# Sums of the normed x from its two parts, and another order of products in the first layer

## The chip, the cores and the metric

The kernel runs on one core of a Trainium2 chip. The time is device microseconds of one execution, the median of three runs. The profile is of one further execution, whose own time is given below. The engines are called as in the profile: PE is TensorE, PEld its weight load, DVE VectorE, ACT ScalarE, POOL GpSimd, SP SyncE.

## The reference

Two layers on 256 positions of width 1024 in fp32. Each layer has two feed-forward steps (ffa, ffb) with a mixer (attention) between them, and a last norm follows. The change is in the feed-forward steps:

```python
def rms_norm(x, g):
    y = xf * lax.rsqrt(jnp.mean(xf * xf, axis=-1, keepdims=True) + EPS)
    return (y * g.astype(jnp.float32)).astype(x.dtype)

def swiglu(x, w_gate, w_up, w_down):
    return (jax.nn.silu(x @ w_gate) * (x @ w_up)) @ w_down

for l in range(DEPTH):
    x = x + 0.5 * swiglu(rms_norm(x, ffa_norm[l]), ffa_w_gate[l], ffa_w_up[l], ffa_w_down[l])
    x = x + hybrid_mixer(rms_norm(x, mix_norm[l]), ...)
    x = x + 0.5 * swiglu(rms_norm(x, ffb_norm[l]), ffb_w_gate[l], ffb_w_up[l], ffb_w_down[l])
return rms_norm(x, final_norm)
```

The gate and up matrices are 1024 x 2816, the down matrix is 2816 x 1024.

## The kernel before

Every fp32 operand is split in a high and a low part. The high part is a rounded copy that ScalarE makes (whi at L300, xhi at L413, hhi at L557), the low part is the rest, which VectorE subtracts (wlo at L279, xlo at L416, hlo at L559). A product is then three matmuls of 128x512 (L319 to L321): high with high, low with high, high with low.

The feed-forward steps run in the order ffa0, ffb0, ffa1, ffb1, with mix0 and mix1 behind ffa0 and ffa1. "Layer 0" in this document is ffa0, the first of them. At the start of each, x is transposed on TensorE (L407) 128x128 at a time into a bank of PSUM (tb). ScalarE makes xhi from it and VectorE xlo. The kernel also needs the normed x (its gain included, its row factor not) as four plain fp32 blocks of 128x512, called a11, a12, a21, a22. ScalarE copies them out of the same bank by 128x128 (L428), into tiles called p, 16 copies for each of the four steps. Two such blocks are added or subtracted on VectorE (L527), and the results are split again (L531, L533) into "forms" for products 5, 6, 3 and 7.

The gate and up columns are worked in an order that a plan per step gives. A name g0, u0, g2 and so on is a plain block of 512 columns of gate or up, in two halves of the depth (16 products in all); h5 is the last block, 256 columns of each. A name of two digits is one of seven Strassen-like products, the first digit, of a pair of column blocks, the second digit; it has four products. The weights of these are sums, too: products 1, 5, 6, 4 of a column follow each other in one raw tile (3 and 7 in another), and each step adds the next matrix to it by an accumulating DMA from POOL (adder, L255 to L262). Such a DMA may start only when the split of the one before is over. Product 43 is thus 63's tile with one more gate block added. After the plan come the 11 units of the down matrix (d0 to d10).

A planner, class Flow, builds the program: threads ask for events, buffers and times, and it steps whichever is due first by a rough model of the engines' times. What it emits is the program's order, and every engine runs its own list in that order. The splitter (L264 to L298) takes the weights unit by unit, in halves, up to three units ahead of TensorE, since there are six pairs of whi and wlo halves. There are five raw tiles, five p tiles, two tb banks.

The norm's squares (L442) are taken by ScalarE from x, and their factor is computed by VectorE (L346 to L357) and applied later, at the gate.

Of the kernel before, what the change touches and what calls it, by code (L numbers as in the profile page):

```python
# [8 lines left out]
F32 = mybir.dt.float32  # L9
# [3 lines left out]
AF = mybir.ActivationFunctionType  # L13
OP = mybir.AluOpType
AX = mybir.AxisListType

T = 2
D = 1024
KT = D // 128
# [20 lines left out]
ARRIVE = [4.4, 5.2, 6.7, 7.4], [8.9, 9.6, 11.1, 11.8]  # L40
ARRIVE_X = [3.5, 5.9, 8.1, 10.3]
HOP = 0.3
PLANS = ("g0 u0 11 g2 51 21 31 u2 61 71 13 g4 41 53 23 33 u4 63 73 h5 43".split(),) * 4
AC = 0.1
DV = 0.06

# [84 lines left out]
def hybrid_kernel(ctx, tc, x_in, ffa_norm, ffa_w_gate, ffa_w_up, ffa_w_down, mix_norm, w_in,  # L131
# [3 lines left out]
    nc = tc.nc  # L135
# [10 lines left out]
    fl = Flow()  # L146
    NRAW, NW, NP = 5, 6, 5
# [7 lines left out]
    def tbank():  # L155
        return bank("tb", 2)
# [4 lines left out]
    def md(shape, name, bufs):  # L161
        return mid.tile(shape, F32, name=name, tag=name, bufs=bufs)
# [10 lines left out]
    class Raw:  # L173


        def __init__(self, src, a, b, loads=1):
            self.src, self.a, self.b, self.loads = src, a, b, loads
            self.landed = [Event() for _ in range(4)]
            raws.append(self)
# [198 lines left out]
    class Norm:  # L378

        def __init__(self, gi, wide=False, plain=False):
            self.gi, self.wide = gi, wide
            self.xs = (big.tile([128, KT, 256], F32R, name="xhi", tag="xhi"),
                       big.tile([128, KT, 256], F32R, name="xlo", tag="xlo"))
            self.rs = small.tile([128, T], F32, name="rs", tag="rs", bufs=4)
            self.ss = small.tile([128, 2, T], F32, name="ss2", tag="ss2")
            if wide:
                self.rsb = mid.tile([128, 256], F32, name="rsb", tag="rsb", bufs=1)
            self.plain = {} if plain else None  # L390
            self.turned = {(k, t): Event() for k in range(KT) for t in range(T)}
            self.scaled, self.spread = Event(), Event()
            self.plained, self.left = Event(), KT * T
            self.count = 0

        def gain(self, k):
# [2 lines left out]
        def turn(self, ks, ts, e=0.0):  # L399

            yield e
            yield fl.get("tb")
            ps = tbank()
            n = 128 * len(ts)
            for i, k in enumerate(ks):
                for t in ts:
                    nc.tensor.transpose(ps[:, i * n + (t - ts[0]) * 128:i * n + (t - ts[0] + 1) * 128],  # L407
                                        x[:, t, k * 128:(k + 1) * 128], ident)
            yield fl.pe(0.44)
            sl = slice(ts[0] * 128, ts[0] * 128 + n)  # L410
            es = []
            for i, k in enumerate(ks):
                nc.scalar.activation(self.xs[0][:, k, sl], ps[:, i * n:(i + 1) * n], AF.Copy, scale=self.gain(k))  # L413
                es.append(fl.act(n))
            for i, k in enumerate(ks):
                nc.vector.scalar_tensor_tensor(self.xs[1][:, k, sl], ps[:, i * n:(i + 1) * n], self.gain(k),  # L416
                                               self.xs[0][:, k, sl].bitcast(F32), op0=OP.mult, op1=OP.subtract)
                e = fl.dve(n, es[i])
                for t in ts:
                    self.turned[k, t].set(e)  # L420
            if self.plain is not None:
                for i, k in enumerate(ks):
                    for t in ts:
                        if (t, k // 4) not in self.plain:
                            yield fl.get("p")
                            self.plain[t, k // 4] = md([128, 512], "p", NP)
                        b = i * n + (t - ts[0]) * 128
                        nc.scalar.activation(self.plain[t, k // 4][:, k % 4 * 128:(k % 4 + 1) * 128],  # L428
                                             ps[:, b:b + 128], AF.Copy, scale=self.gain(k))
                        e = max(e, fl.act(128))  # L430
                        self.left -= 1
                if not self.left:
                    self.plained.set(e)
            fl.put("tb", 0, e)

        def squares(self, t, c, e=0.0):
# [61 lines left out]
    def ffn(us, nm, nxt, plan, last=False):  # L498
# [8 lines left out]
        def event(*k):  # L507
            return evs.setdefault(k, Event())
# [6 lines left out]
        def sums():  # L515

            for k in range(KT):
                for t in range(T):
                    yield nm.turned[k, t]
            yield nm.plained  # L520
            a11, a12, a21, a22 = (nm.plain[t, c] for t in range(T) for c in range(2))
            ho, lo = ([big.tile([128, 4, 256], F32R, name="f" + z, tag=z).rearrange(
                "p a b -> p (a b)").rearrange("p (f n) -> p f n", f=2) for z in tags]
                for tags in (("nhi", "ohi"), ("nlo", "olo")))
            for o, p, q, op in ((a22, a22, a21, OP.subtract), (a21, a11, a21, OP.subtract),
                                (a11, a22, a11, OP.add), (a12, a11, a12, OP.subtract)):
                nc.vector.tensor_tensor(o, p, q, op)  # L527
                yield fl.dve(512)
            for i, (f, z) in enumerate((("5", a22), ("6", a11), ("3", a12), ("7", a21))):
                h, l = ho[i // 2][:, i % 2], lo[i // 2][:, i % 2]  # L530
                nc.scalar.activation(h, z, AF.Copy)  # L531
                yield fl.act(512)
                nc.vector.tensor_tensor(l, z, h.bitcast(F32), OP.subtract)  # L533
                e = fl.dve(512)
                fl.put("p", 0, e)
                forms[f] = [y.rearrange("p (k c) -> p k c", k=4) for y in (h, l)]
                event("form", f).set(e)
# [915 lines left out]
    def finish(t, c, box, g):  # L1453
        if c == 0:
            box["ss"] = small.tile([128, 2], F32, name="ss", tag="ss")
        ss = box["ss"]
        yield fl.get("p")
        junk = md([128, 512], "p", NP)
        nc.scalar.activation(junk, x[:, t, c * 512:(c + 1) * 512], AF.Square, accum_out=ss[:, c:c + 1])
        e = fl.act(512, 0.2)  # L1460
        fl.put("p", 0, e)
        yield e
        if c == 0:
            return
        r = small.tile([128, 1], F32, name="rs1", tag="rs1", bufs=2)
        yield newton([ss[:, :1], ss[:, 1:]], D, r)
        for c in range(2):
            sl = slice(c * 512, (c + 1) * 512)
            yield fl.get("work")
            y = wk([128, 512], "y")  # L1470
            nc.vector.scalar_tensor_tensor(y, x[:, t, sl], r, g[c], op0=OP.mult, op1=OP.mult)
            yield fl.dve(512)
            (nc.sync, nc.scalar)[c].dma_start(out[0, t * 128:(t + 1) * 128, sl], y)
            fl.put("work")
# [6 lines left out]
    units = []  # L1481
    plans = iter(PLANS)
    for i, (kind, _, w) in enumerate(layers):
# [44 lines left out]
    def main():  # L1528
        for i, (kind, _, w) in enumerate(layers):
            last = i + 1 == len(layers)  # L1530
            box = {}

            def nxt(a, c, box=box, i=i, last=last):
                if last:
                    fl.spawn(finish(a, c, box.setdefault(a, {}), box["g"]))
                else:
                    if len(norms) < i + 2:
                        kind2, gi, _ = layers[i + 1]
                        norms.append(Norm(gi, kind2 == "mix", kind2 == "ff" and any(
                            z[0] in "1234567" for z in units[i + 1][1])))  # L1540
                    fl.spawn(norms[i + 1].pair(a, c))

            def gains_out(box=box):
                box["g"] = []
                for c in range(2):
                    yield fl.get("p")
                    g = md([128, 512], "p", NP)
                    nc.gpsimd.dma_start(g, bass.AP(tensor=final_norm.tensor, offset=final_norm.offset + 512 * c,
                                                   ap=[[0, 128], [1, 512]]))
                    box["g"].append(g)  # L1550

            if kind == "ff":
                us, plan = units[i]
                yield from ffn(us, norms[i], nxt, plan, gains_out if last else None)
            else:
                yield from mixer(w, units[i], norms[i], nxt)
            while not last and len(norms) < i + 2:
                yield fl.clock + 0.5
# [5 lines left out]
    def warm():  # L1564
# [5 lines left out]
            fl.pe(0.215)  # L1570
            yield fl.clock
        fl.put("acc")
    norms = [Norm(0, False, any(z[0] in "1234567" for z in units[0][1]))]
    fl.spawn(warm(), 9)
    fl.spawn(turn_gains(*gr))
    for q in range(4):
# [43 lines left out]
```

## Time and profile before

| | |
|---|---|
| median of three runs | 1027.48 us (1026.64 to 1027.61) |
| profiled execution | 1027.06 us, span 1025.3 us |
| granted TensorE clock, mean | 0.996 of full |
| PE, DVE, ACT busy | 97%, 71%, 61% of the span |

The page gives shares over the whole span. What the waits are worth is seen in the timeline of one engine, where each row has its start, its duration, and in brackets how long the engine was idle ahead of it and what ended that. Matmuls overlap, so the distance of two starts, not the duration, tells how fast they run.

### The profile page before, as it was taken

What the parts mean: (1) busy time and instruction counts of PE and PEld (TensorE: products, weight loads), DVE (VectorE), ACT (ScalarE), POOL (GpSimd) and SP (SyncE); (2) the same over time, 40 slices, a digit from 0 to 9 for tenths busy, and PEclk for the clock granted to TensorE, in tenths of its full rate; (3) what the DMA queues carried; (4) which work ended last, traced back from release to release, by engine and by line L of the source; (5) the groups of instructions that cost most, each with busy time, mean ns of one, the idle gap of its engine ahead of it and who ended that gap; (6) DMA issues with size and microseconds to landing.
All of it is one profiled execution on the core that took longest, in us unless ns stands there. A gap on an engine that the chain in (4) does not pass through costs nothing.

```text
span 1025.3 us, 14273 instructions
## 1 busy us (share of the span) xinstructions
PE 999.1 (97%) x5276; PEld 827.0 (81%) x5276; DVE 730.7 (71%) x1367; ACT 621.2 (61%) x1105; POOL 53.5 (5%) x61
## 2 busy tenths in 40 slices
PE   8999999999999999999989999999999989999996
PEld 6788888898876788888878888888978768788885
DVE  5978854688786868784477778447888768688544
ACT  7766543569575866653376566336795767665431
POOL 1110000100000010100001110001000001110000
PEclk9999999999999999999999999999999999999998
DMA  9799965363732599975539998653655237999611
GB/s 327 216 280 258 278 240 180 114 195 109 280 124 82 151 264 291 265 262 198 171 121 229 285 274 266 199 168 111 206 195 175 84 106 224 267 268 303 222 67 41
DMA packets 100983, 207.63 MB, mean 203 GB/s; under 512 B 3785, under 2 KB 23377, under 8 KB 100913
## 3 DMA queue, kind: packets, MB, share of 16 engines
q1 hardware_dynamic: 83072, 171.65, 48.3%
q0 software_dynamic: 17536, 34.54, 19.0%
q8 instruction: 41, 0.67, 0.3%
q10 hardware_dynamic: 304, 0.53, 0.1%
q14 instruction: 30, 0.24, 0.1%
HBM read 205.66 MB, written 1.05 MB: 202 GB/s over the span
## 4 chain that ended last, share of the span: by engine, by line
PE 80%; DVE 8%; ACT 5%; DMA 5%; issue 2%; DVEq 0%; POOL 0%; ACTq 0%; POOLq 0%
PE acc L319 16%; PE acc L320 15%; PE acc L321 15%; PE sb L319 6%; PE sb L321 6%; PE sb L320 6%; DVE wlo L279 3%; DMA raw<-in_ffb_w_up_dram 3%; PE acc L336 2%; PE acc L337 2%; PE acc L338 2%; DMA raw<-in_ffa_w_up_dram 2%; PE acc L1081 2%; PE tb L552 2%; PE tb L1063 2%
## 5 line engine op out<-in xcount | busy, mean ns | idle before, releaser
L279 DVE TENSOR_TENSOR wlo<-raw,whi 128x1024 fp32r<-128x1024 f32 (+2 forms) x404 | 449.8, 1138 | 191.0 <-ACT whi L300 190.4
L300 ACT ACTIVATE whi<-raw 128x1024 fp32r<-128x1024 f32 (+2 forms) x404 | 388.4, 989 | 240.3 <-PE acc L321 89.8
L319 PE MATMUL acc<-whi,hhi 128*128 128x512 f32 x352 | 138.5, 394 | 0.0
L321 PE MATMUL acc<-whi,hlo 128*128 128x512 f32 x352 | 137.4, 390 | 0.0
L320 PE MATMUL acc<-wlo,hhi 128*128 128x512 f32 x352 | 137.1, 390 | 0.0
L320 PE MATMUL acc<-wlo,xhi 128*128 128x512 f32 (+1 forms) x320 | 123.5, 386 | 7.5 <-DVE wlo L279 7.4
L319 PE MATMUL acc<-whi,xhi 128*128 128x512 f32 (+1 forms) x320 | 126.8, 396 | 1.4 <-ACT whi L300 1.4
L319 PE MATMUL sb<-whi,xhi 128*128 128x512 f32 x320 | 125.5, 392 | 0.0
L321 PE MATMUL sb<-whi,xlo 128*128 128x512 f32 x320 | 124.8, 390 | 0.0
L320 PE MATMUL sb<-wlo,xhi 128*128 128x512 f32 x320 | 124.7, 390 | 0.0
L321 PE MATMUL acc<-whi,xlo 128*128 128x512 f32 (+1 forms) x320 | 122.7, 383 | 0.1
L320 PEld LDWEIGHTS acc<-wlo,xhi 128*128 128x128 f32 x320 | 60.7, 190 | 20.7 <-DVE wlo L279 11.1
L321 PEld LDWEIGHTS acc<-whi,hlo 128*128 128x128 f32 x352 | 66.1, 188 | 13.9
L320 PEld LDWEIGHTS acc<-wlo,hhi 128*128 128x128 f32 x352 | 66.2, 188 | 13.4
L319 PEld LDWEIGHTS acc<-whi,hhi 128*128 128x128 f32 x352 | 66.1, 188 | 13.2
L319 PEld LDWEIGHTS acc<-whi,xhi 128*128 128x128 f32 x320 | 60.6, 189 | 12.4 <-ACT whi L300 1.9
L321 PEld LDWEIGHTS acc<-whi,xlo 128*128 128x128 f32 x320 | 60.5, 189 | 12.2 <-DVE xlo L416 0.9
L321 PEld LDWEIGHTS sb<-whi,xlo 128*128 128x128 f32 x320 | 60.1, 188 | 12.6
L320 PEld LDWEIGHTS sb<-wlo,xhi 128*128 128x128 f32 x320 | 60.1, 188 | 12.3
L319 PEld LDWEIGHTS sb<-whi,xhi 128*128 128x128 f32 x320 | 60.1, 188 | 12.2
L336 PE MATMUL acc<-xhi,whi 128*128 128x256 f32 x192 | 56.5, 294 | 0.0
L337 PE MATMUL acc<-xlo,whi 128*128 128x256 f32 x192 | 54.3, 283 | 0.0
(221 smaller groups left out, 1434.5 us busy)
## 6 DMA issues: line engine op xcount, KB each, us to landing
raw<-in_ffa_w_down_dram SPq DMA_DIRECT2D x22, 1024.0 KB, 5.1
raw<-in_ffb_w_down_dram SPq DMA_DIRECT2D x22, 1024.0 KB, 5.1
raw<-in_w_in_dram SPq DMA_DIRECT2D x20, 1024.0 KB, 5.1
raw<-in_ffb_w_gate_dram SPq DMA_DIRECT2D x20, 1024.0 KB, 5.2
raw<-in_ffa_w_gate_dram SPq DMA_DIRECT2D x18, 1024.0 KB, 7.7
raw<-in_ffa_w_up_dram SPq DMA_DIRECT2D x16, 1024.0 KB, 6.1
raw<-in_ffb_w_up_dram SPq DMA_DIRECT2D x16, 1024.0 KB, 7.0
raw<-in_ffa_w_up_dram POOLq DMA_DIRECT2D x12, 1024.0 KB, 9.2
```

The source lines that it names most:

```text
L279: nc.vector.tensor_tensor(view(u, lo, i, True), source(u, i), view(u, hi.bitcast(F32), i, True), OP.subtract)
L300: nc.scalar.activation(view(u, u.halves[-1][0], i, True), source(u, i), AF.Copy)
L319: nc.tensor.matmul(ps, xh, wh, start=first, stop=False, skip_group_check=True)
L320: nc.tensor.matmul(ps, xh, wl, start=False, stop=False, skip_group_check=True)
L321: nc.tensor.matmul(ps, xl, wh, start=False, stop=last, skip_group_check=True)
L336: nc.tensor.matmul(ps, wh, xs[0][:, k], start=first and j == 0, stop=False, skip_group_check=True)
L337: nc.tensor.matmul(ps, wh, xs[1][:, k], start=False, stop=False, skip_group_check=True)
L338: nc.tensor.matmul(ps, wl, xs[0][:, k], start=False, stop=last, skip_group_check=True)
L552: nc.tensor.transpose(ps[:, j * 128:(j + 1) * 128], h[:, j * 128:(j + 1) * 128], ident)
L1063: nc.tensor.transpose(ps[:, j * 128:(j + 1) * 128], pp[:, i * n + s_ * 128:i * n + (s_ + 1) * 128], ident)
L1081: nc.tensor.matmul(grp.o[u * 64:(u + 1) * 64, h // 2 * 128:(h // 2 + 1) * 128], val(s_), pT[:, j * 128:(j + 1) * 128], start=u not in grp. ...
```

## The change

ScalarE's 16 plain copies per step (L428 before) are gone, and with them the events that told when they were done. Instead, when all of x is split and the norm's factor is computed, VectorE adds xhi and xlo, 128x512 at a time, into the four p tiles (L514 after). The tb bank is released straight after xlo. The plan of layer 0 differs from that of the other three, where all four had been alike: g2 comes ahead of product 11, and the blocks u2, g4, u4 and h5 each take the place of the next, so that h5 stands ahead of 63.

```diff
-PLANS = ("g0 u0 11 g2 51 21 31 u2 61 71 13 g4 41 53 23 33 u4 63 73 h5 43".split(),) * 4
+PLANS = ("g0 u0 g2 11 u2 51 21 31 g4 61 71 13 u4 41 53 23 33 h5 63 73 43".split(),) + (
+    "g0 u0 11 g2 51 21 31 u2 61 71 13 g4 41 53 23 33 u4 63 73 h5 43".split(),) * 3
...
-            if self.plain is not None:
-                for i, k in enumerate(ks):
-                    for t in ts:
-                        if (t, k // 4) not in self.plain:
-                            yield fl.get("p")
-                            self.plain[t, k // 4] = md([128, 512], "p", NP)
-                        b = i * n + (t - ts[0]) * 128
-                        nc.scalar.activation(self.plain[t, k // 4][:, k % 4 * 128:(k % 4 + 1) * 128],
-                                             ps[:, b:b + 128], AF.Copy, scale=self.gain(k))
-                        e = max(e, fl.act(128))
-                        self.left -= 1
-                if not self.left:
-                    self.plained.set(e)
             fl.put("tb", 0, e)
...
-            yield nm.plained
-            a11, a12, a21, a22 = (nm.plain[t, c] for t in range(T) for c in range(2))
+            yield nm.scaled
+            yield fl.clock + 1.0
+            blocks = []
+            for t in range(T):
+                for c in range(2):
+                    yield fl.get("p")
+                    a = md([128, 512], "p", NP)
+                    h, l = (z[:, 4 * c:4 * c + 4, t * 128:(t + 1) * 128].bitcast(F32) for z in nm.xs)
+                    nc.vector.tensor_tensor(a.rearrange("p (k c) -> p k c", k=4), h, l, OP.add)
+                    yield fl.dve(512)
+                    blocks.append(a)
+            a11, a12, a21, a22 = blocks
```

The first place is ScalarE's list at the program's start, where g0's weights are split in pieces of 128x512 between the pieces of x. Before:

```order
L300 ACTIVATE whi<-raw 128x512
L413 ACTIVATE xhi<-tb,gall 128x256 x2
L428 ACTIVATE p<-tb,gall 128x128 x4
L300 ACTIVATE whi<-raw 128x512
L413 ACTIVATE xhi<-tb,gall 128x256 x2
L428 ACTIVATE p<-tb,gall 128x128 x4
L300 ACTIVATE whi<-raw 128x512 x2
L413 ACTIVATE xhi<-tb,gall 128x256 x2
L428 ACTIVATE p<-tb,gall 128x128 x4
L300 ACTIVATE whi<-raw 128x512 x2
L413 ACTIVATE xhi<-tb,gall 128x256 x2
L428 ACTIVATE p<-tb,gall 128x128 x4
```

After, in the same place:

```order
L301 ACTIVATE whi<-raw 128x512
L412 ACTIVATE xhi<-tb,gall 128x256 x2
L301 ACTIVATE whi<-raw 128x512
L412 ACTIVATE xhi<-tb,gall 128x256 x2
L301 ACTIVATE whi<-raw 128x512 x3
L412 ACTIVATE xhi<-tb,gall 128x256 x2
L301 ACTIVATE whi<-raw 128x512 x2
L412 ACTIVATE xhi<-tb,gall 128x256 x2
L301 ACTIVATE whi<-raw 128x512
L428 ACTIVATE junk,ss_101<-x 128x512 x2
```

The p copies are gone, and the squares (junk) follow the last whi of g0.

The second place is VectorE's list on the border ffb0 to ffa1: x gets its last additions from ffb0 (L726 before, L722 after), and the wlo rows in the midst are of g0. Before:

```order
L726 SCALAR_TENSOR_TENSOR x<-acc,x 128x512
L416 SCALAR_TENSOR_TENSOR xlo<-tb,gall,xhi 128x128 x4
L726 SCALAR_TENSOR_TENSOR x<-acc,x 128x512
L416 SCALAR_TENSOR_TENSOR xlo<-tb,gall,xhi 128x128 x4
L726 SCALAR_TENSOR_TENSOR x<-acc,x 128x512 x2
L279 TENSOR_TENSOR wlo<-raw,whi 128x1024
L416 SCALAR_TENSOR_TENSOR xlo<-tb,gall,xhi 128x128 x8
L279 TENSOR_TENSOR wlo<-raw,whi 128x1024
```

After:

```order
L722 SCALAR_TENSOR_TENSOR x<-acc,x 128x512
L415 SCALAR_TENSOR_TENSOR xlo<-tb,gall,xhi 128x128 x4
L722 SCALAR_TENSOR_TENSOR x<-acc,x 128x512
L415 SCALAR_TENSOR_TENSOR xlo<-tb,gall,xhi 128x128 x4
L722 SCALAR_TENSOR_TENSOR x<-acc,x 128x512 x2
L280 TENSOR_TENSOR wlo<-raw,whi 128x1024
L415 SCALAR_TENSOR_TENSOR xlo<-tb,gall,xhi 128x128 x4
L280 TENSOR_TENSOR wlo<-raw,whi 128x1024
L415 SCALAR_TENSOR_TENSOR xlo<-tb,gall,xhi 128x128 x4
L280 TENSOR_TENSOR wlo<-raw,whi 128x1024
```

The second of these splits of g0 now stands ahead of the last four xlo, and no longer behind them.

The third place is VectorE's list at the end of layer 0's plan. Before, the single wlo behind L642 is the first half of 43, and the first of the three behind L647 the second:

```order
L279 TENSOR_TENSOR wlo<-raw,whi 128x1024
L637 TENSOR_TENSOR p<-acc,p 128x512
L642 TENSOR_TENSOR z<-acc,p 128x512
L279 TENSOR_TENSOR wlo<-raw,whi 128x1024
L647 SCALAR_TENSOR_TENSOR z<-z,neg,sg 128x512
L279 TENSOR_TENSOR wlo<-raw,whi 128x1024 x3
```

After, the wlo behind L583 is the first half of 43, and the one behind the first hlo (L555) its second; L628 to L643 make the product z of column 3 out of its banks:

```order
L583 SCALAR_TENSOR_TENSOR sg<-sb,rs,sg 128x256 x2
L280 TENSOR_TENSOR wlo<-raw,whi 128x1024
L628 TENSOR_TENSOR p<-p,acc 128x512
L630 TENSOR_TENSOR p<-p 128x512
L555 TENSOR_TENSOR hlo<-tb,hhi 128x2x128
L280 TENSOR_TENSOR wlo<-raw,whi 128x1024
L555 TENSOR_TENSOR hlo<-tb,hhi 128x2x128
L633 TENSOR_TENSOR p<-acc,p 128x512
L638 TENSOR_TENSOR z<-acc,p 128x512
L280 TENSOR_TENSOR wlo<-raw,whi 128x1024
L643 SCALAR_TENSOR_TENSOR z<-z,neg,sg 128x512
```

The evacuations L628 and L630 and a hlo now stand between the two halves of 43, where only L647 stood.

## Rows read from the trace of the kernel before

**Rows 1.** Busy time, share of the span and instructions of each engine, from the page.
```profile
PE 999.1 (97%) x5276; PEld 827.0 (81%) x5276; DVE 730.7 (71%) x1367; ACT 621.2 (61%) x1105; POOL 53.5 (5%) x61
```

**Rows 2.** Groups by line: operation, count | busy us, mean ns | idle us before.
```profile
L428 ACT ACTIVATE p<-tb,gall 128x128 f32<-128x128 f32 x64 | 18.2, 368 | 19.7 <-DVE xlo L416 19.7
...
L527 DVE TENSOR_TENSOR p<-p 128x512 f32<-128x512 f32 x16 | 11.0, 686 | 0.3
```

**Rows 3.** ScalarE's timeline, first block: start us, us, engine, line, operation, shapes, idle before.
```profile
17.97 1.14 ACT L428 ACTIVATE p<-tb,gall 128x128 f32<-128x128 f32 x4 [0.94 <-DVE xlo L416]
18.98 1.16 ACT L300 ACTIVATE whi<-raw 128x512 fp32r<-128x512 f32 x2
```

**Rows 4.** TensorE's timeline over the first block, layer 0.
```profile
8.21 0.48 PE L319 MATMUL acc<-whi,xhi 128*128 128x512 f32 x1
...
19.68 0.50 PE L319 MATMUL acc<-whi,xhi 128*128 128x512 f32 x1 [1.44 <-ACT whi L300]
...
23.95 0.39 PE L320 MATMUL acc<-wlo,xhi 128*128 128x512 f32 x1
24.18 0.39 PE L321 MATMUL acc<-whi,xlo 128*128 128x512 f32 x1
```

**Rows 5.** TensorE's waits on the border mix0 to ffb0: total us, times, longest.
```profile
PE acc L320 <- DVE wlo L279: 2.2, 3, 1.3
PE tb L407 <- DVE x L1419: 0.9, 1, 0.9
```

**Rows 6.** TensorE's timeline behind that border, one stall.
```profile
335.73 0.39 PE L319 MATMUL acc<-whi,xhi 128*128 128x512 f32 x1
336.51 0.50 PE L320 MATMUL acc<-wlo,xhi 128*128 128x512 f32 x1 [0.40 <-DVE wlo L279]
```

**Rows 7.** TensorE's timeline, border ffb0 to ffa1.
```profile
524.50 0.50 PE L320 MATMUL acc<-wlo,xhi 128*128 128x512 f32 x1 [2.73 <-DVE wlo L279]
```

**Rows 8.** Stretch behind it: length, busy PE, PEld, DVE, ACT, POOL, granted clock, DMA, GB/s.
```profile
524.50:528.70 4.20, 4.20 (x11) 3.32 (x12) 3.72 (x15) 3.56 (x6) 0.00 (x0) 0.59 0.72 235
```

**Rows 9.** ScalarE's timeline, border ffb0 to ffa1.
```profile
515.13 2.02 ACT L300 ACTIVATE whi<-raw 128x1024 fp32r<-128x1024 f32 x2
...
519.37 1.14 ACT L428 ACTIVATE p<-tb,gall 128x128 f32<-128x128 f32 x4 [1.20 <-DVE xlo L416]
...
521.00 1.15 ACT L413 ACTIVATE xhi<-tb,gall 128x128 fp32r<-128x128 f32 x4
```

**Rows 10.** VectorE's timeline, border ffb0 to ffa1.
```profile
522.19 1.13 DVE L416 SCALAR_TENSOR_TENSOR xlo<-tb,gall,xhi 128x128 fp32r<-128x128 f32 x4 [2.85 <-ACT xhi L413]
523.23 1.22 DVE L279 TENSOR_TENSOR wlo<-raw,whi 128x1024 fp32r<-128x1024 f32 x1
```

**Rows 11.** VectorE's timeline, splits of u4 and of product 63 in layer 0.
```profile
103.16 3.50 DVE L279 TENSOR_TENSOR wlo<-raw,whi 128x1024 fp32r<-128x1024 f32 x3 [0.30 <-ACT whi L300]
```

**Rows 12.** VectorE's timeline, last sum of x in the layer ffa1.
```profile
539.09 0.68 DVE L533 TENSOR_TENSOR folo<-p,fohi 128x512 fp32r<-128x512 f32 x1
```

**Rows 13.** DMA issues from 106.9 to 122 us: KB each, us to landing.
```profile
raw<-in_ffa_w_down_dram SPq DMA_DIRECT2D x2, 1024.0 KB, 8.1
raw<-in_ffa_w_gate_dram POOLq DMA_DIRECT2D x1, 1024.0 KB, 14.6
```

**Rows 14.** TensorE's timeline, starts of products 33 and 43, layer 0.
```profile
100.56 0.39 PE L319 MATMUL acc<-whi,fohi 128*128 128x512 f32 x1
...
131.87 0.39 PE L319 MATMUL acc<-whi,xhi 128*128 128x512 f32 x1
```

**Rows 15.** DMA issues of the whole span from POOL: KB each, median us to landing.
```profile
raw<-in_ffa_w_up_dram POOLq DMA_DIRECT2D x12, 1024.0 KB, 9.2
raw<-in_ffa_w_gate_dram POOLq DMA_DIRECT2D x4, 1024.0 KB, 12.9
```

**Rows 16.** VectorE's timeline, evacuations of column 3, layer 0.
```profile
119.61 0.69 DVE L634 TENSOR_TENSOR p<-p 128x512 f32<-128x512 f32 x1
120.21 0.68 DVE L559 TENSOR_TENSOR hlo<-tb,hhi 128x512 fp32r<-128x512 f32 x1
```

More of the change, by code (lines that the diff above doesn't have):

```diff
@@ L378, in hybrid_kernel, with __init__ @@
     class Norm:
-        def __init__(self, gi, wide=False, plain=False):
+        def __init__(self, gi, wide=False):
             self.gi, self.wide = gi, wide
@@ L389, in __init__ @@
                 self.rsb = mid.tile([128, 256], F32, name="rsb", tag="rsb", bufs=1)
-            self.plain = {} if plain else None
             self.turned = {(k, t): Event() for k in range(KT) for t in range(T)}
             self.scaled, self.spread = Event(), Event()
-            self.plained, self.left = Event(), KT * T
             self.count = 0
@@ L1538, in nxt @@
                         kind2, gi, _ = layers[i + 1]
-                        norms.append(Norm(gi, kind2 == "mix", kind2 == "ff" and any(
-                            z[0] in "1234567" for z in units[i + 1][1])))
+                        norms.append(Norm(gi, kind2 == "mix"))
                     fl.spawn(norms[i + 1].pair(a, c))
@@ L1572, in warm @@
         fl.put("acc")
-    norms = [Norm(0, False, any(z[0] in "1234567" for z in units[0][1]))]
+    norms = [Norm(0)]
     fl.spawn(warm(), 9)
```

## The prediction

> **What bounds the kernel now.** First I read the page's busy line: TensorE is busy for 97% of the span, VectorE for 71%, ScalarE for 61% [rows 1]. So the time is TensorE's own work and the few gaps in it, and only a change that closes or opens a gap there counts. Next I read the groups of instructions for what the change takes away: 64 copies at L428, 368 ns each, and 19.7 us in which ScalarE stood idle before them, 16 times, always until VectorE's xlo was done [rows 2]. Then I went through TensorE's timeline for gaps and looked whether such a copy stands ahead of each on ScalarE. They stand ahead at four places: the first block (g0) of layer 0, and the three later borders into a feed-forward layer.
>
> At the start a group of four copies waits 0.94 us and takes 1.02 us until the next instruction (17.97 to 18.98); only then come the last two splits of g0's weights [rows 3]. TensorE waits 1.44 us for the first of these at 19.68 and ends g0 at about 24.4 [rows 4]. On the borders from a mixer TensorE waits for wlo and x, 3.1 us [rows 5]. A wait costs more than itself: the matmul of 336.51 starts 0.78 after its neighbour, where undisturbed ones stand 0.23 apart, so 0.55 for a wait of 0.40 [rows 4, 6]. On the border ffb0 to ffa1 the wait is 2.73 us [rows 7], and the granted clock then stands at a mean of 0.59 for 4.2 us [rows 8], most of it at the lower of its two levels (1.2 GHz; 1.00 is 2.4 GHz).
>
> **What the change removes.** At the start: the three groups from 10.26, 14.11 and 17.97 cost 1.96 us each of ScalarE (wait and copies) [rows 3], 5.9 together. The last whi of g0, which ended at 20.15 (18.98 and two instructions of 1.17), can then end at about 14.3, unless the loads of g0 and x come later. TensorE itself needs, from 8.21, 16 products of 3 x 0.2275 = 10.9 and two remaining sets of transposes, 0.9: 20.0 at the earliest. I leave 0.7 for waits on those loads: 20.7 against 24.4, **gain 3.7** (bounds 2.5 and 4.4).
>
> On a mixer border the four stalls (0.93, 0.40, 1.34, 0.51 on the timeline) are 3.1 of wait and some 0.15 to 0.2 each for the restart, 3.9. In the new order ScalarE reaches the second half of g0's second half-block about 4 us sooner, since groups of 1.0 and their waits of about 1.2 [rows 9] are gone; following ScalarE and VectorE by hand through the new order, each split is ready 1 us or more before its product. A rest of 0.3 to 0.4 stays for the transposes: **gain 3.5 each, twice** (bounds 1.5 and 3.9).
>
> On ffb0 to ffa1 the chain is: copies behind xlo (519.37) hold the next xhi to 521.00 [rows 9]; the xlo of it ends at 523.3, and only then comes wlo (523.23), whose whi had been there since 517.2 [rows 9, 10]; TensorE starts at 524.50. In the new order wlo stands ahead of these four xlo, and xhi comes some 2 us sooner, with nothing to wait for. The wait of 2.73, its restart 0.1, and the slow clock, 4.2 x 0.41 = 1.7, go: 4.5, less 0.2, **gain 4.3** (bounds 2.5, if the clock still falls, and 4.5).
>
> **What it adds.** Four additions per layer on VectorE. The nearest row is the 128x512 addition at L527, 686 ns [rows 2], so 2.7 us per layer. They stand after the norm's factors, one between two splits. A split half takes 1.14 there (the three at 103.16 show it [rows 11]), with an addition 1.8, while TensorE uses up a half in 4 products, 2.7; so the splits still gain on TensorE. The sums that they feed were ready at 539.8 [rows 12], when TensorE still had over 10 us of plain blocks ahead of product 51 (at 524.50 it was in the first of three blocks of 10.9). I take 0; without cover it would be 2.7 a layer. For transposes that the planner put a little too early I take a loss of 0.6 (0 to 1.5).
>
> **The new plan in layer 0.** The first Strassen product moves behind g2, which adds nothing: the same products, each 2.73. But at the end 43 now follows 73 directly; before, h5 (10.9 us) lay between. The weights of 43 are a sum: its DMA from POOL may start only when 63's split is over. Before, that was 106.66 [rows 11], the transfer took 14.6 us [rows 13], so it landed at about 121.5, and TensorE came to 43 at 131.87 [rows 14]: 8 us to spare with the split still to do. They are now gone. Product 33 started at 100.56 [rows 14]; u4 now lies ahead of it (+10.9) and the start is 3.7 sooner: about 108.1 with small losses. Then 33, h5, 63, 73: 2.73 + 10.92 + 2.73 + 2.73, so 43 is due at 127.2 to 127.7. Its sum is issued at about 114.0 (63's split ends 5 to 6 after 33's start, as before). The gate sums took 12.9 in the middle, up's 9.2 [rows 15]; by the gate rows, of which 43's own is the longest, I take 13.6, landing at 127.6. Then whi 1.05 and wlo 1.2: first half at 129.9, 2.2 late.
>
> More is queued behind it. On VectorE two additions of column 3, and a 256-wide hlo stand between 43's two halves; at 0.6, 0.6 (119.61 to 120.21 [rows 16]) and 0.35, and 1.14 for the split, the second half comes 2.7 after the first, where TensorE needs it 1.4 after. Behind that stand hlo, two more evacuations, the split of d0 and the product z, whose transposes TensorE takes straight after 43: 0.35 + 0.6 + 0.6 + 1.14 + 0.7, so 6.1 after the first half, at 136.0, against 130.4 had nothing waited: 5.5 lost. With pauses of that length the clock may fall as at 524.5; I add 1.0. **Loss 6.5** (0.5 with a transfer of 9.2; 9 with 14.6, a late 63 and 1.7 for the clock).
>
> In the trace two loads of the down weights are issued while 43's sum is under way; it takes 14.6, and the gate sums 12.9 in the middle, against 9.2 for up's [rows 13, 15]. The Trainium skill, in "DMA: Bandwidth & Descriptors", section "Queues, rings and completion order", says that each DMA engine takes turns between the queues that have work for it, packet by packet. By this rule the sum gives turns to the down weights as long as their loads are in flight, which speaks for the long figure, a loss of 6.5, and against the change; without it the short figure, a loss of 0.5, would be the one to take. The rows of gate agree with the rule.
>
> **Sum.** 3.7 + 2 x 3.5 + 4.3 - 0.6 - 6.5 = 7.9. The profiled execution took 1027.06 (span 1025.3), which gives 1019.2; the median of the runs, 1027.48, lies 0.4 above it. I say 1019.4.
>
> **Rivals.**
> 1. The sum for 43 lands quickly (9.2 to 11): loss 0.5 to 2 in place of 6.5, time 1013.6 to 1015.1. For it: up's sums. Against: the gate rows are long [rows 15], and loads of the down weights are still in flight. Chance 0.22.
> 2. VectorE, not ScalarE, sets the borders: the xlo and splits come in nearly the same order, so only half of the 15.0 is won, 7.5, and 43 still costs 6.5 and the small waits 0.6: 1027.1, no change that can be measured. For it: at 523.23 the wait was for wlo behind xlo [rows 10]. Against: that xlo itself waited for xhi behind the copies [rows 9]. Half-way forms of this give 1022 to 1025. No change: 0.09.
> 3. Slower: 43 costs more than all is worth. Place: end of layer 0's gate and up phase; from the sum's landing on, each us of delay is one us of TensorE. It outweighs the 14.4 by 2 when the sum takes about 23 us, with 1.7 for the clock (130.4 less 2.3 and 6.1 for the split and its queue is 122.0; 16.4 less 1.7 later is 136.7); then 1029.5 and more. For it: ScalarE and VectorE run in order, so that d0's weights wait behind 43's too. Against: the longest seen is 14.6 [rows 13]. Chance 0.05.
> 4. The copies were hidden anyway and TensorE's gaps stay: then only the losses are left, 1034.6. Against it stands every gap read above; chance 0.02.
>
> **Numbers.** The forecast (1016 to 1023) has 0.62, rival 1 0.22, rival 2 0.09, rivals 3 and 4 0.07. Less than 0.2% (2 us) cannot be told from no change here. Faster 0.84, same 0.09, slower 0.07. The range reaches from rival 1's middle to the half-way forms of rival 2: 1013 to 1024.5; the forecast's own is 1016 to 1023.
>
> **What will show it.** Right: g0 of layer 0 ends near 20.7; no wait over 0.5 us for wlo within 20 us of the three borders; the granted clock at full after ffb0; at about 127 to 136 in layer 0 waits for 43's wlo and for z, and the sum's transfer at 12 us or more. Wrong: no wait there (rival 1), waits for wlo at the borders with xhi long there (rival 2), or product 51 waiting for its sums.

## The result, and the profile after

The changed kernel takes 1013.94 us (median of four runs, 1013.52 to 1014.65) against 1027.06 us; the ratio is 0.9873, with a 95% interval of 0.9856 to 0.9890. The forecast was 1019.4, range 1013 to 1024.5: right in direction and within the range, at its low end, 5.5 us above what was measured and outside the forecast's own 1016 to 1023. The number is that of rival 1, but its mechanism did not happen.

The page's busy line of the changed kernel, the answer to [rows 1]:

```profile
PE 994.3 (98%) x5270; PEld 826.1 (82%) x5270; DVE 739.1 (73%) x1383; ACT 604.1 (60%) x1041; POOL 53.5 (5%) x61
```

ScalarE works 17 us less, VectorE 8 more. All of TensorE's waits of the changed kernel (total us, times, longest), where the kernel before had, among others, those of [rows 5] twice and that of [rows 7]:

```profile
PE acc L320 <- DVE p L633: 5.7, 1, 5.7
PE acc L321 <- DVE wlo L280: 1.6, 2, 0.8
PE acc L1564 <- POOL ident masks.py:199: 1.4, 1, 1.4
PE tb L406 <- DVE xlo L415: 0.6, 1, 0.6
PE acc L1337 <- ACT m L307: 0.4, 2, 0.2
```

One wait is left that matters: 5.7 us for L633, and it is new. The two of 0.8 at L321 stand in the mixers' output products, in both kernels.

At the start TensorE's rows, to set beside [rows 4], are

```profile
7.55 0.48 PE L320 MATMUL acc<-whi,xhi 128*128 128x512 f32 x1
...
19.92 0.39 PE L320 MATMUL acc<-whi,xhi 128*128 128x512 f32 x1
```

g0 ends at 19.92 in place of 24.4, and ScalarE's last split of it begins at 13.05, where the last two ran from 18.98 on [rows 3]. Ahead of it stands xhi, and no group of copies:

```profile
12.34 0.82 ACT L412 ACTIVATE xhi<-tb,gall 128x256 fp32r<-128x256 f32 x2
13.05 0.63 ACT L301 ACTIVATE whi<-raw 128x512 fp32r<-128x512 f32 x1
```

On the border ffb0 to ffa1, VectorE's rows, to set beside [rows 10]:

```profile
513.01 1.13 DVE L415 SCALAR_TENSOR_TENSOR xlo<-tb,gall,xhi 128x128 fp32r<-128x128 f32 x4 [0.45 <-ACT xhi L412]
514.05 1.22 DVE L280 TENSOR_TENSOR wlo<-raw,whi 128x1024 fp32r<-128x1024 f32 x1
515.60 1.13 DVE L415 SCALAR_TENSOR_TENSOR xlo<-tb,gall,xhi 128x128 fp32r<-128x128 f32 x4 [0.33 <-ACT xhi L412]
516.64 1.22 DVE L280 TENSOR_TENSOR wlo<-raw,whi 128x1024 fp32r<-128x1024 f32 x1
```

The xlo waits 0.45 and 0.33 us for xhi, where one waited 2.85, and the splits stand between the groups of xlo. Stretches of TensorE behind two borders (length, busy PE, PEld, DVE, ACT, POOL, granted clock, DMA share, GB/s), to set beside [rows 8]:

```profile
510.50:527.00 16.50, 16.50 (x78) 13.67 (x77) 15.26 (x34) 12.49 (x23) 0.00 (x0) 1.00 0.47 150
322.00:345.00 23.00, 22.88 (x109) 18.77 (x109) 19.51 (x51) 17.40 (x36) 0.00 (x0) 1.00 0.49 158
128.00:136.00 8.00, 4.90 (x15) 3.93 (x16) 7.72 (x11) 3.25 (x4) 0.00 (x0) 0.57 0.46 138
```

TensorE is busy for all of the first and nearly all of the second, at a granted clock of 1.00. The third stretch is the price of the new plan: product 43 in layer 0, where TensorE is busy for 4.9 of 8.0 us and the clock stands at 0.57, near its lower level of 1.2 GHz. Its rows on TensorE:

```profile
125.01 0.39 PE L322 MATMUL acc<-whi,folo 128*128 128x512 f32 x1
131.10 0.76 PE L320 MATMUL acc<-whi,xhi 128*128 128x512 f32 x1 [5.71 <-DVE p L633]
131.66 0.63 PE L321 MATMUL acc<-wlo,xhi 128*128 128x512 f32 x1
132.09 0.63 PE L322 MATMUL acc<-whi,xlo 128*128 128x512 f32 x1
```

and on VectorE:

```profile
126.01 1.22 DVE L280 TENSOR_TENSOR wlo<-raw,whi 128x1024 fp32r<-128x1024 f32 x1 [5.54 <-ACT whi L301]
127.15 0.68 DVE L628 TENSOR_TENSOR p<-p,acc 128x512 f32<-128x512 f32 x1
127.86 0.69 DVE L630 TENSOR_TENSOR p<-p 128x512 f32<-128x512 f32 x1
128.47 0.42 DVE L555 TENSOR_TENSOR hlo<-tb,hhi 128x256 fp32r<-128x256 f32 x1
128.81 1.21 DVE L280 TENSOR_TENSOR wlo<-raw,whi 128x1024 fp32r<-128x1024 f32 x1
129.94 0.42 DVE L555 TENSOR_TENSOR hlo<-tb,hhi 128x256 fp32r<-128x256 f32 x1
130.28 0.68 DVE L633 TENSOR_TENSOR p<-acc,p 128x512 f32<-128x512 f32 x1
```

73 ends at 125.24 and 43 begins at 131.10, and the starts then stand 0.43 apart, not 0.23. The sum for 43 was issued at 111.78, and took, beside a load of the down weights (to set beside [rows 13]):

```profile
raw<-in_ffa_w_gate_dram POOLq DMA_DIRECT2D x1, 1024.0 KB, 13.1
raw<-in_ffa_w_down_dram SPq DMA_DIRECT2D x1, 1024.0 KB, 8.2
```

So the first half of 43 was split at 127.1, 1.9 late. But TensorE did not start then. 43 accumulates in the bank where 73 has just been, and L633 must have read it first; L633 needs only the end of 73, but stands on VectorE behind both halves of 43's split. The wait ends with L633, at 130.9.

### The profile page after: what moved, and what is told of

Same layout as the page of the kernel before. It is cut to its first block, busy times and chain, and to the rows that moved or that the text cites. A ratio compares the mean times of both kernels' runs of the same rounds, so it can differ in the third digit from the quotient of the medians.

```text
span 1012.5 us, 14210 instructions
## 1 busy us (share of the span) xinstructions
PE 994.3 (98%) x5270; PEld 826.1 (82%) x5270; DVE 739.1 (73%) x1383; ACT 604.1 (60%) x1041; POOL 53.5 (5%) x61
## 3 DMA queue, kind: packets, MB, share of 16 engines
HBM read 205.66 MB, written 1.05 MB: 204 GB/s over the span
## 4 chain that ended last, share of the span: by engine, by line
PE 90%; DMA 4%; DVE 3%; ACT 2%; issue 1%; DVEq 0%; POOL 0%; ACTq 0%; POOLq 0%
PE acc L320 18%; PE acc L321 18%; PE acc L322 18%; PE sb L322 6%; PE sb L320 6%; PE sb L321 6%; DMA raw<-in_ffb_w_up_dram 3%; PE acc L337 2%; PE acc L338 2%; PE acc L339 2%; PE acc L1077 2%; PE tb L548 2%; PE tb L1059 2%; DVE wlo L280 1%; DMA raw<-in_ffa_w_gate_dram 1%
## 5 line engine op out<-in xcount | busy, mean ns | idle before, releaser
L320 PE MATMUL acc<-whi,xhi 128*128 128x512 f32 (+1 forms) x336 | 133.1, 396 | 5.7 <-DVE p L633 5.7
L321 PE MATMUL acc<-wlo,hhi 128*128 128x512 f32 x352 | 137.0, 389 | 0.0
L321 PE MATMUL acc<-wlo,xhi 128*128 128x512 f32 (+1 forms) x336 | 128.9, 383 | 0.0
L322 PE MATMUL acc<-whi,xlo 128*128 128x512 f32 (+1 forms) x336 | 128.5, 382 | 0.0
L320 PE MATMUL sb<-whi,xhi 128*128 128x512 f32 x304 | 119.2, 392 | 0.0
L322 PE MATMUL sb<-whi,xlo 128*128 128x512 f32 x304 | 118.4, 390 | 0.0
L321 PE MATMUL sb<-wlo,xhi 128*128 128x512 f32 x304 | 118.3, 389 | 0.0
L320 PEld LDWEIGHTS acc<-whi,xhi 128*128 128x128 f32 x336 | 63.7, 189 | 17.2 <-ACT whi L301 6.1
L321 PEld LDWEIGHTS acc<-wlo,hhi 128*128 128x128 f32 x352 | 66.1, 188 | 13.5
L322 PEld LDWEIGHTS acc<-whi,xlo 128*128 128x128 f32 x336 | 63.6, 189 | 12.3
L321 PEld LDWEIGHTS acc<-wlo,xhi 128*128 128x128 f32 x336 | 63.7, 190 | 10.7 <-DVE wlo L280 0.2
L322 PEld LDWEIGHTS sb<-whi,xlo 128*128 128x128 f32 x304 | 57.0, 188 | 12.0
L321 PEld LDWEIGHTS sb<-wlo,xhi 128*128 128x128 f32 x304 | 57.1, 188 | 11.7
```

Of the source, the lines that this page charges most:

```text
L320: nc.tensor.matmul(ps, xh, wh, start=first, stop=False, skip_group_check=True)
L321: nc.tensor.matmul(ps, xh, wl, start=False, stop=False, skip_group_check=True)
L322: nc.tensor.matmul(ps, xl, wh, start=False, stop=last, skip_group_check=True)
```

## Experiments

Every run was timed against the kernel before on the same chip, in three rounds; the kernel before came out at 1027.06 to 1027.54 in them. "The change" below is the changed kernel, 1013.94. Distances between two traces are taken from the starts of TensorE's products.

**Only the new plan.** The kernel before with the change's `PLANS`:

```diff
-PLANS = ("g0 u0 11 g2 51 ... 33 u4 63 73 h5 43".split(),) * 4
+PLANS = ("g0 u0 g2 11 u2 ... 33 h5 63 73 43".split(),) + ("g0 u0 11 g2 ... h5 43".split(),) * 3
```

> The kernel before with only the new order of products in layer 0; ScalarE still makes the plain copies. Theory (the new order costs what 43 waits for, about 7.5 us with the slow clock behind it, and saves nothing here): TensorE waits 4 to 6 us at product 43 and the time is 1033 to 1036. Rival (the new order is worth something by itself, because its first sums are asked for later): 1024 to 1027.

1032.28 us, ratio 1.0052 [1.0036, 1.0069]: 5 us slower, a little below the 1033 of the theory. TensorE waits at 43 as in the change, for the same evacuation (L638 here):

```profile
136.44 0.77 PE L320 MATMUL acc<-whi,xhi 128*128 128x512 f32 x1 [4.91 <-DVE p L638]
```

The wait's 4.91, with its restart and the slow clock, is 7.0. The 2 us less than that have a reason: between 25 and 130 us TensorE has no wait in this run, where the kernel before has these (total us, times, longest):

```profile
PE tb L552 <- DVE sg L577: 0.9, 2, 0.7
PE tb L552 <- DVE z L647: 0.5, 1, 0.5
```

So the new order does save something, 1.4 us of waits and their restarts, 2.1 by the distances. It costs more: behind g0, layer 0 is 4.9 longer.

The rest of the difference between the two spans (1030.6 and 1025.3) is not the plan's work. Up to the end of g0 the three engines have the same lists in both, and TensorE waits for the same split at the same time, 1.47 us here and 1.44 before [rows 4]. Yet g0 ends 1.6 later here, because the granted clock fell behind the wait, which it did not do before. The row and the stretch here, then the stretch before:

```profile
19.69 0.49 PE L320 MATMUL acc<-whi,xhi 128*128 128x512 f32 x1 [1.47 <-ACT whi L301]
20.90:24.30 3.40, 3.40 (x10) 2.64 (x9) 2.62 (x5) 3.40 (x8) 0.00 (x0) 0.51 0.96 314
```

```profile
20.90:24.30 3.40, 3.40 (x17) 2.67 (x15) 2.61 (x5) 3.40 (x8) 0.00 (x0) 1.00 1.01 346
```

On the border ffb0 to ffa1 it is the other way round: the wait of [rows 7] is there with 2.75 us, and the clock of [rows 8] is 1.00 and not 0.59:

```profile
530.93 0.50 PE L321 MATMUL acc<-wlo,xhi 128*128 128x512 f32 x1 [2.75 <-DVE wlo L280]
530.93:535.13 4.20, 4.20 (x18) 3.30 (x18) 3.71 (x15) 3.56 (x6) 0.00 (x0) 1.00 0.72 230
```

So the same wait can bring the slow clock in one execution and not in another, and some 1.7 us between two single traces can be that alone.

**Only the additions.** The changed kernel with the old plan in all four steps:

```diff
-PLANS = ("g0 u0 g2 11 u2 ... 33 h5 63 73 43".split(),) + ("g0 u0 11 g2 ... h5 43".split(),) * 3
+PLANS = ("g0 u0 11 g2 51 ... 33 u4 63 73 h5 43".split(),) * 4
```

> The changed kernel with the old order of products in layer 0, so that h5 lies between 73 and 43 again. Theory (the wait at 43 goes, and the sums of x are just in time for product 51, which now comes 11 us sooner): no wait at 43, up to 3 us at 51, time 1006 to 1010. Rival (without the new order product 51 waits for its sums, as they now come after the factors of the norm): 5 us or more at 51, 1013 or more.

1008.69 us, ratio 0.9825 [0.9810, 0.9839], 5.2 us better than the change. No wait at 43 and none at 51; the waits in layer 0's plan are

```profile
PE tb L547 <- DVE z L642: 1.5, 1, 1.5
PE tb L547 <- DVE sg L572: 0.3, 1, 0.3
```

The sum for 43 takes 14.0 us in this run, and with h5 ahead of 43 nobody waits for it. The rival is out: the sums of x are in time for 51 in the old plan, too. What the additions alone gain, 18.6 us, less what the plan alone costs, 5.0, is 13.6; the change has 13.1.

**The planner told of the late sum.** Same work, other order around 43:

```diff
-                e.set(loader.last + 2.0)
+                e.set(loader.last + (8.0 if j == 7 else 2.0))
```

(j counts the sums; 7 is 43 of layer 0.)

> The changed kernel; the planner alone is told that 43's sum in layer 0 lands 6 us later, so it puts the evacuations of column 3 ahead of 43's split on VectorE and ScalarE. Theory (of the 5.7 us wait at 43 only 2 are the late weights, and the rest is the evacuation L633, which stood behind both halves' splits): wait of 2 us or less, little or no slow clock, time 1008 to 1010.5. Rival (the landing of the sum sets it): 1013 to 1015.

1011.01 us, ratio 0.9842 [0.9827, 0.9856]: 2.9 us of the 7.7 that 43 costs come back, less than the theory's 3.4 to 5.9 and more than the rival's none. L633 now stands ahead of the split, at 125.83:

```profile
125.83 0.69 DVE L633 TENSOR_TENSOR p<-acc,p 128x512 f32<-128x512 f32 x1 [0.91 <-PE acc L322]
...
127.83 2.35 DVE L280 TENSOR_TENSOR wlo<-raw,whi 128x1024 fp32r<-128x1024 f32 x2
```

But the planner also put the transposes of z ahead of 43 on TensorE, and these wait for L643:

```profile
128.05 0.63 PE L548 MATMUL tb<-ident,z 128*128 128x128 f32 x4 [2.26 <-DVE z L643]
128.44 0.47 PE L320 MATMUL acc<-whi,xhi 128*128 128x512 f32 x1
```

The wait is 2.26, and the granted clock then stands at 0.61 in this stretch:

```profile
129.00:133.40 4.40, 4.30 (x12) 3.42 (x13) 4.05 (x5) 4.10 (x5) 0.00 (x0) 0.61 0.46 134
```

So the order behind a late transfer is worth 2.9 us here; it does not make the weights themselves earlier.

**A quiet sum.** The changed kernel; d0, d1 and d2 of layer 0 are loaded from POOL behind 43's sum (`downs` lists the loads of the down matrices, `issued[7]` is the event that 43's sum is issued):

```diff
+            behind = u in downs[:3]
+            if behind:
+                yield issued[7]
...
-                    nc.sync.dma_start(dst[:, i * k:(i + 1) * k], u.src[:, i * k:(i + 1) * k])
+                    (nc.gpsimd if behind else nc.sync).dma_start(dst[:, i * k:(i + 1) * k], u.src[:, i * k:(i + 1) * k])
```

> The changed kernel; in layer 0 the loads of d0, d1 and d2 are issued from POOL behind 43's sum and not from SP beside it, so that the sum has the DMA engines nearly to itself. Theory (the loads beside it make it long): it lands in 8 to 10 us and not 13, the wait at 43 falls from 5.7 to 1 to 1.5 (L633 must still read the bank when 73 is done), no slow clock, time 1007 to 1009.5. Rival (a sum of a gate matrix is long by itself): 12 us or more, time 1013 to 1015.

1008.41 us, ratio 0.9818 [0.9801, 0.9834]. The sum lands in 8.4 us and not in 13.1:

```profile
raw<-in_ffa_w_gate_dram POOLq DMA_DIRECT2D x1, 1024.0 KB, 8.4
```

and product 43 starts after 1.05 us:

```profile
126.92 0.47 PE L326 MATMUL acc<-whi,xhi 128*128 128x512 f32 x1 [1.05 <-DVE p L639]
127.23 0.40 PE L327 MATMUL acc<-wlo,xhi 128*128 128x512 f32 x1
127.47 0.39 PE L328 MATMUL acc<-whi,xlo 128*128 128x512 f32 x1
```

Its weights are there (split at 123.0 and 125.8), and what is left is the wait for L633 (L639 in this run), which cannot start before 73 has ended and has a hlo of 0.4 us ahead of it. The clock stays up: the next start is 0.31 later, and 0.24 the one after. This is the theory in full. The Trainium skill, "DMA: Bandwidth & Descriptors", section "Queues, rings and completion order", has each DMA engine take turns, packet by packet, between the queues with work. The run agrees: 8.4 us without a second queue's loads, 13.1 with them.

**The copies back, from the bank.** The changed kernel, additions on VectorE, and in Norm.turn again 16 copies per step behind xlo, into a tile that nobody reads (`copied` is set in the feed-forward steps, `scratch` is a single tile of 128x128):

```diff
+            if self.copied:
+                for i, k in enumerate(ks):
+                    for t in ts:
+                        b = i * n + (t - ts[0]) * 128
+                        nc.scalar.activation(scratch, ps[:, b:b + 128], AF.Copy, scale=self.gain(k))
+                        e = max(e, fl.act(128))
```

> The changed kernel with the 64 copies put back on ScalarE behind xlo, out of the tb bank, into a scratch tile that nobody reads; the additions stay on VectorE. Theory (the copies, by their work and by their wait for xlo, made the gaps at the start and on the three borders): the gaps of the kernel before return there, 14 to 18 us, time 1028 to 1032. Rival (VectorE's order of xlo and splits made them): 1014 to 1018.

1040.88 us, ratio 1.0134 [1.0112, 1.0155]: the gaps return, and more than was expected, by some 9 us.

But these are not quite the copies of the kernel before. They all write one tile and do not overlap: at the same 367 ns each, a group of four takes 1.47 us of ScalarE's list until the next instruction, where it took 1.01, and the 64 keep it busy for 23.5 us (the line is below) in place of 18.2 [rows 2]. The planner also moves other work with them: on the border ffb0 to ffa1, VectorE's list is that of the kernel before again, with the second split of g0 behind the last xlo.

**The copies back, from SBUF.** The same, in the same order on TensorE and VectorE, but read from xhi:

```diff
-                        nc.scalar.activation(scratch, ps[:, b:b + 128], AF.Copy, scale=self.gain(k))
+                        nc.scalar.activation(scratch, self.xs[0][:, k, t * 128:(t + 1) * 128].bitcast(F32), AF.Copy, scale=self.gain(k))
```

> The same 64 copies in the same places of the same order, but out of xhi in SBUF and not out of the tb bank, so that they need not wait for anything on VectorE. Theory (each group costs its work of 1.0 us and its wait of about 1.2, and both count): about half of the gaps return, 1020 to 1025. Rival 1 (only the wait for xlo counts): 1014 to 1017. Rival 2 (only the place in the order counts, which is that of the run with the tb bank): as that run.

1023.20 us, ratio 0.9962 [0.9947, 0.9977], as the theory had it. ScalarE's group in the two runs (count | busy, mean ns | idle before), first from the bank:

```profile
L426 ACT ACTIVATE scratch<-tb,gall 128x128 f32<-128x128 f32 x64 | 23.5, 367 | 21.8 <-DVE xlo L417 20.3
```

then from SBUF:

```profile
L426 ACT ACTIVATE scratch<-xhi,gall 128x128 f32<-128x128 f32 x64 | 25.9, 404 | 1.6
```

From SBUF the work is 2.4 us more and the idle time 20.2 less, and the kernel is 17.7 us faster. So of the 27 us that the copies cost here, the 9.3 over the change are at most what their work and the changed lists cost; 2.3 us of wait for the load of x at the start are in this trace, too. The other 17.7 come with reading the bank. The copies wait for xlo, which reads the same bank; they also hold the bank, for which TensorE waits 1.3 us at the start; and behind the longer waits the granted clock fell to 0.50 three times (14.3 to 17.7, 342.0 to 345.4, 536.5 to 539.9), where it stays at 1.00 in the run from SBUF. TensorE's waits for wlo are 8.8 us from the bank and 5.5 from SBUF; from the bank, then from SBUF:

```profile
PE acc L322 <- DVE wlo L281: 8.8, 8, 3.8
PE tb L408 <- ACT scratch L426: 1.3, 1, 1.3
```

```profile
PE acc L322 <- DVE wlo L281: 5.5, 6, 1.3
```

The Trainium skill, "PSUM — Partial Sum Buffer", section "PSUM bank collisions raise a hardware error", says that reads by ScalarE and VectorE of one bank must not overlap and that the compiler's scheduler orders them. The rows show such an order: 16 waits until xlo's end from the bank, none from SBUF.

That the run from the bank came out beyond 1032 is settled in part. Between the last product of one feed-forward step and the down matrix of the next it is slower than the run with the plan alone by 1.9, 2.0 and 1.1 us on the three later steps. Each of these has four groups that take 0.46 us longer than those of the kernel before, and on the first two the clock fell as said, which it did not there in the run with the plan alone. The trace is that of its fastest execution, 1038.27; no trace shows the 2.6 us from there to the median, and no run shows whether the additions are still free on top of such gaps.

**The additions twice.** Each addition is done two times:

```diff
-                    nc.vector.tensor_tensor(a.rearrange("p (k c) -> p k c", k=4), h, l, OP.add)
-                    yield fl.dve(512)
+                    for _ in range(2):
+                        nc.vector.tensor_tensor(a.rearrange("p (k c) -> p k c", k=4), h, l, OP.add)
+                        yield fl.dve(512)
```

> The changed kernel with each of the 16 additions of xhi and xlo done twice, 11 us more of VectorE in all. Theory (VectorE has room there): 1013.5 to 1015.5, and no new wait. Rival (VectorE is the limit on these borders): 2.7 us more per layer, 1020 to 1025.

1014.99 us, ratio 0.9883 [0.9868, 0.9897] against the kernel before, 1.05 us above the change; the two intervals overlap. VectorE does 11 us more at 686 ns each, and nearly all of it is covered. Two waits stand in this trace that the change's does not have, one for sg in layer 0, and one for the load of x at the start, ahead of the first addition:

```profile
PE tb L549 <- DVE sg L574: 0.9, 1, 0.9
PE tb L406 <- DMA x<-in_x_dram: 0.9, 2, 0.8
```

The wait at 43 is shorter in it, 5.2 and not 5.7. So at most the first can be put down to the additions, and a cost of 1 us is not shown.

**Old plan, tables later.** The kernel of "only the additions", with the mixer's tables begun at 125 us of the planner's clock and not at 40:

```diff
-        yield 40.0
+        yield 125.0
         yield from tables()
```

> The changed kernel with the old order of products in layer 0, and the mixer's tables (VectorE work that the planner spreads over layer 0 from 40 us on) begun at 125 us. Theory (they delayed the product z of column 1, for which TensorE waited 1.55 us at 78): that wait goes and nothing else comes, 1006.5 to 1007.8, against 1008.7 with the old order alone. Rival (the wait is for the chain of column 1 itself): 1008 to 1009.5.

1007.19 us, ratio 0.9806 [0.9792, 0.9821]. The wait of 1.5 us for z is gone from TensorE's waits, and none came for it in layer 0. The interval overlaps that of the old plan alone, so the step of 1.5 us rests on the trace, and there the spans differ by 0.4 only, since g0 ends 0.8 later in this one; from there to the down matrix layer 0 is 2.2 us shorter. Against the change the gain is 6.7 us, and this is the lowest median of the study, though its interval overlaps that of the quiet sum as well.

## Why the prediction was right in direction and short in size

The spans differ by 12.8 us (1025.3 and 1012.5). By the distances between TensorE's rows in the two traces the steps of the sum measured:

| step | forecast | measured |
|---|---|---|
| start, end of g0 | +3.7 | +4.5 |
| the mixer borders | +3.5 each | +4.2, +4.2 |
| ffb0 to ffa1 | +4.3 | +4.6 |
| small waits, and what the plan saves | -0.6 | +3.0 |
| product 43 | -6.5 | -7.7 |

**The start.** The copies' 1.96 us a group was the right price: the last split moved from half a microsecond behind 18.98 to 13.05, by 6.4 us. I kept 0.7 for loads; there was no such wait (the 0.6 for xlo at L406 lies ahead of g0), and g0 itself began 0.66 sooner, since TensorE had waited 0.86 for the load of x in the trace before. Part of this is luck: in the six traces whose lists start as the change's, g0 ends 3.6 to 4.5 sooner than before.

**The borders.** ScalarE, not VectorE, set them, and rival 2 is out: the two runs with copies put back have one and the same list on VectorE, and differ by 17.7 us by where ScalarE's copies read. From SBUF 3.0 of the 4.6 us of the border ffb0 to ffa1 stay won, though VectorE's list there is that of the kernel before; what VectorE's order has in the other 1.6, beside the copies' work, is not shown. The rest of 0.2 to 0.4 that I held back for transposes is not there. What the sum had as one price (copies of 1.0 and waits of 1.2) is two, and the two runs show that both count; their shares in the kernel before stay open, since the copies put back are longer. Of the 4.6 on ffb0 to ffa1, 1.7 is the slow clock of [rows 8], which I took as sure to be there before; the run with only the new plan has the same wait without it.

**The additions.** The price of 0 held; doubled, they brought 1.05 us, which is not told apart from nothing.

**The step that failed** is the sentence that the new plan "adds nothing" but what 43 loses, and with it the "loss of 0.6" for early transposes. The kernel before had small waits in the middle of steps, for sg and z, which I did not put in any term. The new plan takes 2.2 us of them in layer 0 (the run with the plan alone shows none between 25 and 130 us), and a wait for sg in ffb1 is gone, too, 0.9 by the distances:

```profile
894.19 1.31 PE L552 MATMUL tb<-ident,sg 128*128 128x128 f32 x8 [0.99 <-DVE sg L577]
```

Why the latter went is open; with the plan alone, which leaves ffb1 as it was, it is 0.4. With the 0.6 that was not lost, these make up 3.6 of the 4.9 us by which the sum of 7.9 fell short.

**Product 43.** The sum's landing was forecast well: 13.1 us for 13.6, first half 1.9 late for 2.2. The size was nearly right as well, but not the place. I had 43 start with its weights and z's transposes wait behind it; in fact 43 itself waited, for L633, because 73 and 43 share a bank. I had followed the weights and the queue behind them, and not the bank. By the rows, late weights alone make 1.9 of the wait, and the queue on VectorE the rest; the clock took 1.9 where I had 1.0.

**Rival 1** gave the measured time by a quick sum. The sum was not quick, so its number is right by chance: the start, the borders and the waits that I left out gave 6.1 us more than said and 43 took 1.2 more, and what is left of the two led there.

## What to carry to other kernels

A cheap copy out of a PSUM bank can cost more by what it waits for than by its work (here 17.7 us against at most 9.3): look what else reads the bank, and whether the same value can be had from SBUF on an engine with room. Before an order of products is changed, look at every sum that is built by an accumulating transfer, count what still lies between its start and its use, and list what is queued behind it on each engine that works in order. When a sum of terms is made from a trace, the small waits that the change may take away belong in it just as the large ones do, and a slow clock behind a wait belongs in it with a chance, not as sure.

## What the runs showed of the hardware that was not expected

An accumulating transfer of 1 MB took 13.1 us beside loads on the other queue and 8.4 with those loads behind it on its own queue. That gave 5.5 us, about as much as the old order of products (5.2) and more than the other order behind the late transfer (2.9).

The length of a wait did not decide whether the granted clock fell behind it. It fell behind waits of 1.47, 2.26 and 2.73 us, and it did not behind 1.05, 1.44 and 2.75; 1.44 and 1.47 are the same wait in two runs, and so are 2.73 and 2.75.

Four copies of 128x128 from a PSUM bank took 1.01 us of ScalarE's list where they wrote four places and 1.47 where all wrote one tile, at the same 0.37 us each.
